# Both feed-forward products by one level of Strassen's algorithm, in two phases through device memory, on one Trainium2 core

## The chip, the core and the metric

One core of a Trainium2 chip. The metric is the device time of one execution in microseconds: the median of three runs. A separate execution was taken by the hardware profiler; its rows are what is read here. TensorE does the matmuls, VectorE and ScalarE the elementwise work and the copies out of PSUM, POOL (GpSimd) the weight sums, and SP issues nearly all transfers.

## The reference, cut to what matters

One layer of a streaming encoder: a first half (adaptive norm, input projection, pooling mixer, state-space mixer, output projection, residual), then a squared-ReLU feed-forward with its own norm and residual, then a final norm. Only the feed-forward changes:

```python
h = rms_norm(x, norm_ffn_w) * (1.0 + sc2) + sh2
f = jnp.square(jax.nn.relu(h @ w_ff1 + b_ff1)) @ w_ff2 + b_ff2
x = x + g2 * f
y = rms_norm(x, final_norm_w)
```

D_MODEL is 1024 and the feed-forward is 4096 wide. There are 2048 prompt tokens and 8 x 16 sample tokens, 2176 in all, and everything is float32.

## The kernel before, in words

**Layout and precision.** Features lie on the 128 partitions, tokens along the free dimension. Every matrix product is done in three matmuls of reduced-width operands: `mm3` (L178 to L180) multiplies the high part of the weights with the high and the low part of the data, and the low part of the weights with the high part of the data. The split of a weight tile into parts is a cast on ScalarE and a subtraction on VectorE (`wsplit`, L172 and L174; `wpair`, L952 and L954), from a raw tile that SP loads (four raw buffers, three split ones).

**Stages.** Phase A (to about 1050 us) does the first half up to the mixers. Then the output projection (`out_proj`, L827) runs over three pairs of token tiles, the last of 128-column sample tokens. In its shadow POOL computes sums and differences of the first feed-forward weights (`combine`, L853): for each of 16 units u and each half of the columns it loads four blocks (L857), does four 256-column operations (L859) and stores four results to device memory (L860), with a single buffer `pp`.

**Feed-forward.** It runs over three pairs of token tiles (364 + 364, 364 + 364, 360 + 360 columns; the last tile holds the sample tokens). A pair's two tiles are the two column halves of the Strassen scheme. `load_h` (L892) makes seven operand sets from the normed input (b11, t3, t1, t2, b21, t4, b22; four tiles each, in high and low parts). `ff1_unit` (L957) makes two feature tiles for both token tiles from seven products of 4 x 3 = 12 matmuls each, 84 in all, instead of the 96 of the plain form. Its evictions go to tiles `e` of the pool `fe`; after ReLU and square they are split again and stay in SBUF. `ff2` (L1010) is plain: for every four feature tiles it goes through eight output tiles and two token tiles with 12 matmuls each and adds the result to the residual `xs` on VectorE (L1021). The two are interleaved: two `ff1_unit`s, then one `ff2` step. After the last step come the sums of squares, `rsqrt_of` (small matmuls L237 and L260), the final scale (L1051) and the stores.

**Order.** The kernel is written in program order, with a list of small tasks (`fill`) that are dropped in between (`filler`, `drain`). A scheduler orders each engine's instructions before the run, by priority and the readiness it expects; on the chip each engine, and each DMA queue, works strictly in that order. The memory of the weight sums is given back just before the feed-forward, and the eviction tiles are placed there:

```python
    hs = load_h(SUPERS[0], rs)
    with tc.high_priority(offset=FPRIO):
        drain()
    pstack.close()
    fe = region("fe")
```

## Time and profile before

| what | value |
|---|---|
| median of three runs | 2995.47 us (2990.91 to 3008.11) |
| the profiled execution | 3008.98 us, of which the span is 3007.2 us |
| TensorE busy | 95% of the span |
| VectorE, ScalarE, POOL busy | 65%, 45%, 6% |
| mean granted TensorE clock | 0.973 |
| transfers | 433.74 MB, 144 GB/s over the span |

Busy shares are averages over stages with different limits. A busy TensorE is not one at its peak, since matmuls overlap: the distance between their starts is what one costs. A window row gives busy time and counts for one stretch; after them stand the granted clock (1.00 is the 2.4 GHz level, 0.50 the 1.2 GHz level), the mean busy share of the 16 DMA engines and GB/s.

### The profile page before, as it was taken

The numbers are of one execution on the slowest core, as the hardware profiler recorded it, in microseconds if no ns is written. First come the engines' busy times: TensorE is split into PE (matmuls) and PEld (weight loads), VectorE is DVE, ScalarE is ACT, GpSimd is POOL, SyncE is SP. The second block draws the span as 40 slices with busy tenths as digits, with TensorE's granted clock in tenths as the row PEclk, the third lists the DMA queues.
The fourth block names the chain that finished last, engine by engine and source line by source line (L and its number), as shares of the span: only waits on it lengthen the run. The fifth ranks groups of instructions, "written<-read, shape, count | busy, mean of one in ns | idle before, by whom it ended". The sixth has DMA issues, their size and how long they took to land.

```text
span 3007.2 us, 45269 instructions
## 1 busy us (share of the span) xinstructions
PE 2859.1 (95%) x17000; PEld 2742.3 (91%) x17000; DVE 1969.7 (65%) x3832; ACT 1348.3 (45%) x2518; POOL 184.2 (6%) x228
## 2 busy tenths in 40 slices
PE   7899999999999899999289999999999999999998
PEld 5799998989989799999179999999999999999997
DVE  7578796778978684643354556685555587555556
ACT  6646455544624233232253444554433465334442
POOL 0000000000000043443400000000000000000000
PEclk9999999999999999999589999999999999999999
DMA  6657443523564677876442233454323245222332
GB/s 231 184 181 220 133 126 111 147 91 119 161 163 142 159 251 247 217 241 211 147 147 91 97 109 110 125 172 134 106 95 108 93 150 171 95 92 95 112 109 76
DMA packets 293836, 433.74 MB, mean 144 GB/s; under 512 B 73008, under 2 KB 199920, under 8 KB 293616
## 3 DMA queue, kind: packets, MB, share of 16 engines
q1 hardware_dynamic: 283888, 397.28, 42.9%
q0 software_dynamic: 9728, 33.56, 3.4%
q8 instruction: 134, 2.20, 0.3%
q14 instruction: 86, 0.70, 0.1%
HBM read 364.88 MB, written 65.85 MB: 143 GB/s over the span
## 4 chain that ended last, share of the span: by engine, by line
PE 73%; DMA 9%; issue 6%; POOL 5%; DVE 4%; ACT 2%; SPq 0%; DVEq 0%; POOLq 0%; ACTq 0%
PE g L180 19%; PE g L178 19%; PE g L179 19%; DMA sD<-pp 4%; POOL pp L859 4%; PE y L180 3%; PE y L178 3%; PE y L179 3%; POOL pp L857 2%; PE y L604 1%; PE t L609 1%; PE y L602 1%; DMA sb<-h 1%; PE t L260 1%; PE t L237 1%
## 5 line engine op out<-in xcount | busy, mean ns | idle before, releaser
L178 PE MATMUL g<-h,wh 128*128 128x384 f32 (+3 forms) x2432 | 814.2, 335 | 56.0 <-ACT e L985 47.6
L179 PE MATMUL g<-h,wh 128*128 128x384 f32 (+3 forms) x2432 | 812.6, 334 | 1.8 <-DVE h L900 1.6
L180 PE MATMUL g<-h,wl 128*128 128x384 f32 (+3 forms) x2432 | 814.0, 335 | 0.0
L178 PE MATMUL g<-c,wh 128*128 128x364 f32 (+3 forms) x1792 | 592.4, 331 | 26.0 <-ACT c L899 15.9
L180 PE MATMUL g<-c,wl 128*128 128x364 f32 (+3 forms) x1792 | 593.7, 331 | 0.8 <-DVE wl L174 0.6
L179 PE MATMUL g<-c,wh 128*128 128x364 f32 (+3 forms) x1792 | 591.1, 330 | 2.3 <-DVE c L900 2.0
L178 PEld LDWEIGHTS g<-h,wh 128*128 128x128 f32 x2432 | 462.6, 190 | 69.9 <-ACT e L985 48.1
L172 ACT CAST wh<-wr 128x1024 fp32r<-128x1024 f32 x290 | 301.9, 1048 | 383.4 <-PE g L179 311.9
L179 PEld LDWEIGHTS g<-h,wh 128*128 128x128 f32 x2432 | 462.6, 190 | 12.2 <-issue 6.8
L174 DVE TENSOR_TENSOR wl<-wr,wh 128x1024 fp32r<-128x1024 f32 x290 | 355.0, 1230 | 178.8 <-ACT wh L172 169.4
L180 PEld LDWEIGHTS g<-h,wl 128*128 128x128 f32 x2432 | 462.3, 190 | 8.7 <-issue 5.9
L952 ACT CAST wh<-wr 128x1024 fp32r<-128x1024 f32 x192 | 180.9, 942 | 458.3 <-PE g L179 341.0
L178 PEld LDWEIGHTS g<-c,wh 128*128 128x128 f32 x1792 | 339.4, 189 | 30.2 <-ACT c L899 17.2
L180 PEld LDWEIGHTS g<-c,wl 128*128 128x128 f32 x1792 | 339.2, 189 | 8.8 <-DVE wl L954 4.9
L179 PEld LDWEIGHTS g<-c,wh 128*128 128x128 f32 x1792 | 339.2, 189 | 3.9 <-DVE c L900 2.9
L954 DVE TENSOR_TENSOR wl<-wr,wh 128x1024 fp32r<-128x1024 f32 x192 | 209.5, 1091 | 154.3 <-ACT wh L952 150.7
L1021 DVE SCALAR_TENSOR_TENSOR c<-g,mod,c 128x364 f32<-128x364 f32 (+2 forms) x256 | 146.0, 571 | 170.9 <-PE g L180 170.6
L178 PE MATMUL y<-c,wh 128*128 128x364 f32 (+3 forms) x608 | 200.2, 329 | 3.1 <-DVE c L1021 3.1
L180 PE MATMUL y<-c,wl 128*128 128x364 f32 (+3 forms) x608 | 200.4, 330 | 1.3 <-DVE wl L174 1.3
L179 PE MATMUL y<-c,wh 128*128 128x364 f32 (+3 forms) x608 | 199.8, 329 | 0.0
L972 ACT ACTIVATE e<-e 128x364 f32<-128x364 f32 (+1 forms) x192 | 95.1, 496 | 77.3 <-DVE e L997 72.4
L1021 DVE SCALAR_TENSOR_TENSOR c<-y,mod,c 128x364 f32<-128x364 f32 (+2 forms) x128 | 73.0, 570 | 85.8 <-PE y L180 85.5
(243 smaller groups left out, 3766.7 us busy)
## 6 DMA issues: line engine op xcount, KB each, us to landing
wr<-wf SPq DMA_DIRECT2D x108, 512.0 KB, 3.5
wr<-sD SPq DMA_DIRECT2D x192, 256.0 KB, 3.2
wr<-win SPq DMA_DIRECT2D x84, 512.0 KB, 4.0
wr<-wf SPq DMA_DIRECT2D x144, 256.0 KB, 2.9
wr<-wada SPq DMA_DIRECT2D x48, 512.0 KB, 5.1
E<-aD SPq DMA_DIRECT2D x34, 512.0 KB, 5.4
x<-xT SPq DMA_DIRECT2D x88, 192.0 KB, 3.4
pp<-wf POOLq DMA_DIRECT2D x64, 256.0 KB, 4.1
```

The source lines that it names most:

```text
L172: S.copy(wh, raw)
L174: V.tensor_tensor(wl, raw, wh.bitcast(F32), op=ALU.subtract)
L178: T_.matmul(out, lhsT=wh, rhs=ah, start=start, stop=False, skip_group_check=more)
L179: T_.matmul(out, lhsT=wh, rhs=al, start=False, stop=False, skip_group_check=more)
L180: T_.matmul(out, lhsT=wl, rhs=ah, start=False, stop=stop, skip_group_check=more)
L237: T_.matmul(pn[:, c:c + 1], lhsT=acc[:, c * P:(c + 1) * P], rhs=ones[:, 0:1], start=True, stop=True)
L857: nc.gpsimd.dma_start(w[:, 2 * i:2 * i + 2], a["wf1"][2 * u + i].rearrange("p (b x) -> p b x", b=2)[:, :, hs])
L859: nc.gpsimd.tensor_tensor(w[:, out], w[:, x], w[:, y], op=op)
L952: S.copy(wh[:, :n], raw[:, :n])
L954: V.tensor_tensor(wl[:, :n], raw[:, :n], wh[:, :n].bitcast(F32), op=ALU.subtract)
L972: S.activation(c, c, AF.Relu)
L1021: V.scalar_tensor_tensor(x1[:, :Tp], pg[:, :Tp], G[:, 0:1], x1[:, :Tp], op0=ALU.mult, op1=ALU.add)
```

## The change

The first product keeps its seven products, and the second gets the same scheme. For this the feed-forward is parted in two phases. Phase one runs all 16 units of `ff1_unit` for all three pairs. After each unit POOL forms the four differences t1 to t4 of its results, and seven tiles go to device memory (`fD`). Phase two runs, for each pair, four chunks of four units: `load_f` brings a chunk's 28 operand tiles back and splits them, and each `ff2_unit` makes seven products (84 matmuls) whose evictions are added up in SBUF over the four chunks; in the last chunk `residual` reloads x, scales and adds, and sums the squares. `final` does the last norm, its pieces mixed into the next pair's first units.

`combine` serves both weights: the second ones are summed in the first phase of pairs 0 and 1, half a unit's sums per unit. The sums' pool `pp` is a region of its own; the temporaries of the projection go to a pool `to`, whose place the eviction tiles `fe` take over. The first operand sets of pair 0 are made before the last two column tiles of the projection. In phase two POOL does the low parts of two of a unit's four weight loads. The weights are repacked on the host so that each of the four blocks of a unit is one 512-column run.

In the diff below, removed lines (the functions printed above show them) and some small helpers are left out: `hraw` loads one tile of x and norms it, `hput` splits it, `late` does both for the sets b21 and b22, `optile` and `actile` hand out tiles of three and two pools in turn.

```diff
+    def right(stack, name):
+        return stack.enter_context(tc.tile_pool(name=name, bufs=1, side="right", reuse_waits=REUSE))
+
+    cstack, ostack = ExitStack(), ExitStack()
+    cls_pool = {c: right(cstack, c) for c in ("c0", "c2")}
     tp2 = region("tpb")
+    pp = region("pp")
+    to = ostack.enter_context(tc.tile_pool(name="to", bufs=1, reuse_waits=REUSE))
...
     def tmp():
-        return tp2.tile([P, TM], F32, tag="m", name="m", bufs=3)
+        return to.tile([P, TM], F32, tag="m", name="m", bufs=3)
...
+    HOPS = ("b11", "t3", "t1", "t2", "t4", "b22", "b21")
...
+    def combine(w, u, half):
         hs = slice(256 * half, 256 * half + 256)
-        w = pool.tile([P, 4, 256], F32, tag="pp", name="pp", bufs=1)
-        for i in range(2):
-            nc.gpsimd.dma_start(w[:, 2 * i:2 * i + 2], a["wf1"][2 * u + i].rearrange("p (b x) -> p b x", b=2)[:, :, hs])
+        t = pp.tile([P, 4, 256], F32, tag="pp", name="pp", bufs=1)
+        nc.gpsimd.dma_start(t, a[w][u][:, :, hs])
         for out, x, y, op in ((3, 2, 3, ALU.add), (2, 0, 2, ALU.subtract), (0, 3, 0, ALU.subtract), (1, 1, 0, ALU.subtract)):
-            nc.gpsimd.tensor_tensor(w[:, out], w[:, x], w[:, y], op=op)
-        nc.gpsimd.dma_start(sD[u][:, :, hs], w)
+            nc.gpsimd.tensor_tensor(t[:, out], t[:, x], t[:, y], op=op)
+        nc.gpsimd.dma_start(sD[w][u][:, :, hs], t)
...
+    def wpair(pool_lo, *srcs):
...
+            eng = nc.gpsimd if pool_lo else V
+            eng.tensor_tensor(wl[:, :n], raw[:, :n], wh[:, :n].bitcast(F32), op=ALU.subtract)
...
+    def products(w, u, hs, T, after, pool_lo=()):
+        src = wset(w, u)
+        ws = {}
+        banks = {}
+        for i, n in enumerate(HOPS):
+            if i % 2 == 0:
+                names = HOPS[i:i + 2]
+                ws.update(zip(names, wpair(i // 2 in pool_lo, *(src[x] for x in names))))
+            b = {"b11": "a", "t2": "a", "t3": "c", "t4": "c", "t1": "b", "b22": "b", "b21": "d"}[n]
+            more = b in banks
+            if not more:
+                banks[b] = obank()
+            out = banks[b][:, :T]
+            wh, wl = ws[n]
+            for q in range(4):
+                sl = slice(q * P, (q + 1) * P)
+                hi, lo = hs[n][q]
+                mm3(out, wh[:, sl], wl[:, sl], hi[:, :T], lo[:, :T], q == 0 and not more, q == 3, more)
+            after(n, out)
+            filler(1)
...
+    def load_h(sup, rs, cls, temp, first):
...
+        def early(q):
+            b11, b12, b22 = hraw(sup, rs, q, 0), hraw(sup, rs, q, 1), hraw(sup, rs, q + 4, 1)
+            hput(hs, cls, "b11", q, b11, T)
+            t1 = temp()[:, :T]
+            V.tensor_tensor(t1, b12, b11, op=ALU.subtract)
...
+            if not first:
+                b21 = hraw(sup, rs, q + 4, 0)
+                V.tensor_tensor(b21, b21, t1, op=ALU.subtract)
+                hput(hs, "c1", "t4", q, b21, T)
+
+        def t4(q):
+            keep[q] = hraw(sup, rs, q + 4, 0)
+            t = temp()[:, :T]
+            hi, lo = hs["t2"][q]
+            V.tensor_tensor(t, keep[q], hi[:, :T].bitcast(F32), op=ALU.subtract)
+            V.tensor_tensor(t, t, lo[:, :T].bitcast(F32), op=ALU.subtract)
+            hput(hs, "c1", "t4", q, t, T)
...
+    def ff1_unit(n, sup, hs, u):
...
+            return fe.tile([P, TF], F32, tag="e", name="e", bufs=9)[:, :T]
...
+        def spill(name, c):
+            DQ.dma_start(fD[n][u][HOPS.index(name)], c)
...
+        def after(name, pg):
...
+            else:
+                c = e["c11"]
+                V.tensor_tensor(c, c, pg, op=ALU.add)
+                put("b11", c)
+                spill("b11", c)
+                t1, t2, t4 = (stage()[:, :T] for _ in range(3))
+                sub(t1, e["b12"], e["b11"])
+                spill("t1", t1)
+                sub(t2, e["b22"], t1)
+                spill("t2", t2)
+                sub(e["b12"], e["b22"], e["b12"])
+                spill("t3", e["b12"])
+                sub(t4, e["b21"], t2)
+                spill("t4", t4)
+
+        products("wf1", u, hs, T, after)
...
+    def load_f(n, c, T):
...
+            DQ.dma_start(raw, fD[n][4 * c + q][HOPS.index(x)])
             S.copy(hi[:, :T], raw)
             V.tensor_tensor(lo[:, :T], raw, hi[:, :T].bitcast(F32), op=ALU.subtract)
...
+    def residual(x, pgs, s, m, acc):
+        T, t0, last, Tp = fdims(s)
+        x1 = stage()
+        xcols(x1, m, t0, T)
+        G, B = MOD(5, m), g2b[:, m, :]
+        S.activation(x1[:, :Tp], x1[:, :Tp], AF.Identity, bias=B[:, 0:1])
+        V.scalar_tensor_tensor(x[:, :Tp], x[:, :Tp], G[:, 0:1], x1[:, :Tp], op0=ALU.mult, op1=ALU.add)
...
+        sq_add(tp2, acc[0], x[:, :T], T, not acc[1])
...
+    def ff2_unit(sup, hs, c, mp, A, accs):
...
+        def into(key, pg):
+            if key in A:
+                V.tensor_tensor(A[key], A[key], pg, op=ALU.add)
+            else:
+                A[key] = actile(T)
+                S.copy(A[key], pg)
...
+        def done(key, j, i):
+            if key != "c11":
+                V.tensor_tensor(A[key], A[key], A["u"], op=ALU.add)
+            residual(A[key], None, sup[j], 2 * mp + i, accs[j])
...
+        products("wf2", 4 * c + mp, hs, T, after, (1, 3))
...
-    out_proj(SUPERS[2], pin2, yin2, range(8))
+    out_proj(SUPERS[2], pin2, yin2, range(6))
     drain()
-    hs = load_h(SUPERS[0], rs)
+    hs, rest = load_h(SUPERS[0], rs, "c2", tmp, True)
+    out_proj(SUPERS[2], pin2, yin2, range(6, 8))
+    drain()
     with tc.high_priority(offset=FPRIO):
-        drain()
-    pstack.close()
+        for fn in rest:
+            fn()
+    ostack.close()
     fe = region("fe")
...
     for n, sup in enumerate(SUPERS):
         nxt = SUPERS[n + 1] if n + 1 < len(SUPERS) else []
...
+        for u in range(16):
+            if n < 2:
+                combine("wf2", 8 * n + u // 2, u % 2)
+            if u == 5 and nxt:
+                rs = load_r(nxt)
+            if u == 9:
+                drain()
+                if nxt:
+                    hn, rest = load_h(nxt, rs, "c2" if n % 2 else "c0", etmp, False)
+            ff1_unit(n, sup, hs, u)
         drain()
...
+    cstack.close()
+    opa, opb = right(ctx, "opa"), right(ctx, "opb")
+    hs, rest = load_f(0, 0, FBS[0])
+    with tc.high_priority(offset=F2PRIO):
+        for fn in rest:
+            fn()
+    for n, sup in enumerate(SUPERS):
...
+        for c in range(4):
+            nxt = (n, c + 1) if c < 3 else (n + 1, 0)
+            if nxt[0] < 3:
+                hn, rest = load_f(*nxt, FBS[SUPERS[nxt[0]][0]])
+                fill.extend(rest)
...
+            for mp in range(4):
+                ff2_unit(sup, hs, c, mp, A[mp], accs)
...
+        fin = final(sup, A, accs)
+        if n < 2:
+            drain()
+            fill[0:0] = fin
+        else:
+            for fn in fin:
+                fn()
```

## Rows read from the trace of the kernel before

**Rows 1.** The page's busy shares by engine.

```profile
PE 2859.1 (95%) x17000; PEld 2742.3 (91%) x17000; DVE 1969.7 (65%) x3832; ACT 1348.3 (45%) x2518; POOL 184.2 (6%) x228
```

**Rows 2.** Windows: busy us (x instructions) of PE, PEld, DVE, ACT, POOL; clock, DMA, GB/s.

```profile
1440.00:1470.00 30.00, 12.87 (x33) 9.21 (x33) 22.24 (x40) 13.40 (x26) 12.13 (x15) 0.50 0.56 173
1470.00:1514.00 44.00, 0.00 (x0) 0.00 (x0) 0.00 (x0) 0.22 (x1) 18.83 (x26) 0.50 0.27 93
...
1514.40:1545.00 30.60, 27.59 (x130) 25.14 (x131) 22.30 (x40) 25.99 (x55) 0.00 (x0) 0.85 0.64 186
...
1600.00:1700.00 100.00, 100.00 (x598) 99.19 (x597) 54.98 (x82) 42.63 (x76) 0.00 (x0) 1.00 0.30 98
...
1900.00:2000.00 100.00, 96.86 (x572) 95.80 (x572) 77.60 (x141) 61.67 (x115) 0.00 (x0) 0.98 0.49 149
2000.00:2100.00 100.00, 96.55 (x563) 94.56 (x561) 65.72 (x117) 50.00 (x93) 0.00 (x0) 0.98 0.49 157
...
2400.00:2500.00 100.00, 97.66 (x573) 96.28 (x573) 80.93 (x154) 62.21 (x117) 0.00 (x0) 0.98 0.45 136
2500.00:2600.00 100.00, 96.00 (x569) 94.40 (x568) 65.96 (x133) 46.89 (x87) 0.00 (x0) 0.98 0.45 145
```

**Rows 3.** Timeline of PE: start us, duration us; the feed-forward's first and last, and neighbours.

```profile
1431.46 0.33 PE L178 MATMUL g<-c,wh 128*128 128x364 f32 x1
...
1700.25 0.33 PE L178 MATMUL g<-c,wh 128*128 128x364 f32 x1
1700.41 0.33 PE L179 MATMUL g<-c,wh 128*128 128x364 f32 x1
1700.58 0.33 PE L180 MATMUL g<-c,wl 128*128 128x364 f32 x1
...
2990.59 0.33 PE L180 MATMUL y<-h,wl 128*128 128x360 f32 x1
```

**Rows 4.** Timeline of ACT around the first eviction; in brackets the idle time before it.

```profile
1513.78 0.56 ACT L985 ACTIVATE e<-g,vec 128x364 f32<-128x364 f32 x1 [48.47 <-DMA sD<-pp]
```

**Rows 5.** The tile view of `pp`: POOL's sums, and what POOL waited for.

```profile
L859 POOL TENSOR_TENSOR pp<-pp x128: 712/745/1707, 1063.9 to 1509.2; 128x256 f32<-128x256 f32 x128
...
  DMA pp<-wf: 128.6, 32
  DMA sD<-pp: 119.4, 31
```

**Rows 6.** Queues at 300:900, 1514:2000, 2000:2510, POOL's at 1050:1420: packets, MB, share.

```profile
q1 hardware_dynamic: 65995, 77.94, 44.3%
...
q1 hardware_dynamic: 35424, 56.36, 36.9%
...
q1 hardware_dynamic: 36864, 60.60, 37.5%
...
q0 software_dynamic: 7456, 25.69, 21.1%
```

**Rows 7.** Chain of waits from 1515 and at the end: start us, us, what.

```profile
1534.87 0.43 SPq L866
...
2023.50 1.14 DVE wl L954
...
2026.60 0.45 DVE acc L276
...
3000.89 3.00 DVE c L1051 x6
```

**Rows 8.** Timeline of DVE near 1450: one op beside a sum of POOL, one alone.

```profile
1446.73 1.06 DVE L294 TENSOR_TENSOR x<-x,rb 128x364 f32<-128x364 f32 x1
...
1455.96 0.53 DVE L900 TENSOR_TENSOR c<-m,c 128x364 fp32r<-128x364 f32 x1
```

**Rows 9.** Timeline of POOL: four sums beside VectorE's ops, four without.

```profile
1445.44 3.92 POOL L859 TENSOR_TENSOR pp<-pp 128x256 f32<-128x256 f32 x4 [4.95 <-DMA pp<-wf]
...
1472.20 3.12 POOL L859 TENSOR_TENSOR pp<-pp 128x256 f32<-128x256 f32 x4 [3.42 <-DMA pp<-wf]
```

More of the change, by code (lines that the diff above doesn't have):

```diff
@@ new lines, in wpair @@
+    def wpair(pool_lo, *srcs):
+        n = 512 * len(srcs)
+        with tc.high_priority(offset=WPRIO):
+            raw = wp.tile([P, 1024], F32, tag="wr", name="wr", bufs=WRB)
+            for i, src in enumerate(srcs):
+                DQ.dma_start(raw[:, 512 * i:512 * i + 512], src)
+            wh = wp.tile([P, 1024], F32R, tag="wh", name="wh")
+            S.copy(wh[:, :n], raw[:, :n])
+            wl = wp.tile([P, 1024], F32R, tag="wl", name="wl")
+            eng = nc.gpsimd if pool_lo else V
+            eng.tensor_tensor(wl[:, :n], raw[:, :n], wh[:, :n].bitcast(F32), op=ALU.subtract)
+        return [(wh[:, 512 * i:512 * i + 512], wl[:, 512 * i:512 * i + 512]) for i in range(len(srcs))]
@@ L893, in load_h, with late @@
+    def load_h(sup, rs, cls, temp, first):
         T = FBS[sup[0]]
         hs = {n: [None] * 4 for n in HOPS}
-        def put(n, q, raw):
-            cls = "c2" if n in ("b11", "t3", "t1") else "c1"
-            hi, lo = qt(cls, F32R), qt(cls, F32R)
+        keep = {}
+        def early(q):
[3 more added lines that the diff above has]
+            V.tensor_tensor(t1, b12, b11, op=ALU.subtract)
+            V.tensor_tensor(b12, b22, b12, op=ALU.subtract)
+            hput(hs, cls, "t3", q, b12, T)
+            hput(hs, cls, "t1", q, t1, T)
+            V.tensor_tensor(t1, b22, t1, op=ALU.subtract)
+            hput(hs, cls, "t2", q, t1, T)
+            if not first:
[9 more added lines that the diff above has]
+            hput(hs, "c1", "t4", q, t, T)
+        def late(n, q):
+            x = keep.pop(q, None) if n == "b21" else None
+            if x is None:
+                x = hraw(sup, rs, q + 4, 1 if n == "b22" else 0)
+            hput(hs, "c1", n, q, x, T)
+        fill.extend(lambda q=q: early(q) for q in range(4))
+        rest = []
+        if first:
+            rest += [lambda q=q: t4(q) for q in range(4)]
+        rest += [lambda n=n, q=q: late(n, q) for n in (("b21", "b22") if first else ("b22", "b21")) for q in range(4)]
+        return hs, rest
@@ new lines, in hymba_step, with optile, actile, one @@
+    nop = [0]
+    def optile():
+        i = nop[0] % 85
+        nop[0] += 1
+        if 53 <= i:
+            return htile()
+        return (opa if i < 33 else opb).tile([P, TF], F32R, tag="op", name="op", bufs=33 if i < 33 else 20)
+    nac = [0]
+    def actile(T):
+        i = nac[0] % 22
+        nac[0] += 1
+        if i < 9:
+            return fe.tile([P, TF], F32, tag="e", name="e", bufs=9)[:, :T]
+        return opb.tile([P, TF], F32, tag="ac", name="ac", bufs=13)[:, :T]
+    def load_f(n, c, T):
+        hs = {x: [None] * 4 for x in HOPS}
+        def one(x, q):
+            lo, hi = optile(), optile()
+            raw = lo[:, :T].bitcast(F32)
+            DQ.dma_start(raw, fD[n][4 * c + q][HOPS.index(x)])
@@ new lines, in one @@
+            hs[x][q] = (hi, lo)
+        return hs, [lambda x=x, q=q: one(x, q) for x in HOPS for q in range(4)]
+    def residual(x, pgs, s, m, acc):
[5 more added lines that the diff above has]
+        V.scalar_tensor_tensor(x[:, :Tp], x[:, :Tp], G[:, 0:1], x1[:, :Tp], op0=ALU.mult, op1=ALU.add)
+        if last:
+            V.tensor_tensor(s3(x[:, Tp:T]), s3(x[:, Tp:T]), strm(G), op=ALU.mult)
+            V.tensor_tensor(s3(x1[:, Tp:T]), s3(x1[:, Tp:T]), strm(B), op=ALU.add)
+            V.tensor_tensor(x[:, Tp:T], x[:, Tp:T], x1[:, Tp:T], op=ALU.add)
+        sq_add(tp2, acc[0], x[:, :T], T, not acc[1])
+        acc[1] = True
@@ new lines, in final, with diag, rows, out @@
+    def final(sup, xs, accs):
+        rs = [None] * len(sup)
+        def diag(j):
+            rs[j] = rsqrt_diag(tp2, accs[j][0], FBS[sup[j]], 1.0 / D, EPS)
+        def rows(j):
+            rs[j] = rsqrt_rows(tp2, rs[j], FBS[sup[j]], direct=sup[j] == FLAST)
+        def out(j, k):
+            T, t0, last, Tp = fdims(sup[j])
+            x = xs[k // 2][f"c{k % 2 + 1}{j + 1}"]
+            V.scalar_tensor_tensor(x, x, VC("fnw", k), rs[j][:, :T], op0=ALU.mult, op1=ALU.mult)
+            DQ.dma_start(o["yT"][:, k, t0:t0 + T], x)
+        js = range(len(sup))
+        return [lambda j=j: diag(j) for j in js] + [lambda j=j: rows(j) for j in js] + \
+               [lambda j=j, k=k: out(j, k) for k in range(KT) for j in js]
@@ L1058, in hymba_step @@
     drain()
-    pstack = ExitStack()
-    pp = pstack.enter_context(tc.tile_pool(name="pp", bufs=1))
     for u in range(16):
         for half in range(2):
-            combine(pp, u, half)
+            combine("wf1", u, half)
     pin1 = in_pool(SUPERS[1], "c2")
```

237 lines of the change are left out of this document (77 added, 160 removed).

## Prediction

> **What bounds the kernel now.** First the busy shares of the page: TensorE has matmuls in flight for 95% of the span [rows 1], so time comes off by fewer matmuls or by closing the few holes, and not by lighter work elsewhere. Then the windows, to find the holes [rows 2]. The reader is to see three kinds of stretch. In a steady one (1600 to 1700) TensorE starts 598 matmuls in 100 us at full clock, VectorE is busy 55 us of it and the DMA engines 0.30. In the hole at the start of the feed-forward (1440 to 1545) there are 33, 0 and 130 matmuls in 30, 44 and 30.6 us, at clock 0.50, 0.50 and 0.85 (0.50 is the 1.2 GHz level). At the two seams between token pairs the counts are 572, 563, 573 and 569. Third the timeline of TensorE, for the price of a matmul [rows 3]: 364-column ones start 0.1667 us apart, so 360-column ones are put at 0.165 by their width.
>
> The feed-forward's matmuls are 3 x 16 x 84 = 4032 in the first product and 3 x 128 x 12 = 4608 in the second; a third of each is 360 wide. That is 5760 x 0.1667 + 2880 x 0.165 = 1435 us. The stretch runs from 1431.5 to 2990.9 [rows 3], 1559 us, so 124 us are lost: 86 at the start (166 matmuls, 27.7 us of work, in the 113.5 us up to 1545), 19 at the two seams (115 matmuls fewer than four times 598), and 19 elsewhere, mostly the norms' own small matmuls.
>
> The start is explained by one wait. ScalarE's first eviction stands 48.5 us until the weight sums' store has landed [rows 4]: its tile `e` lies in the memory that the sums' pool gave back, and the sums run on POOL till 1509, one half-sum per 14.3 us, half of it waits for its own load (128.6 us over 32) and store (119.4 over 31), since there is one buffer [rows 5].
>
> **The change, part by part.** The sum goes against the profiled execution's 3009.0 us (span 3007.2); the median of the runs is 2995.5, 0.9955 of it.
>
> *Fewer matmuls.* The second product gets seven in place of eight: 16 x 84 per pair, 4032 instead of 4608. 8064 matmuls take 5376 x 0.1667 + 2688 x 0.165 = 1340 us: **-96 us**, all on the path.
>
> *The start.* The sums' pool stands by itself now, so no eviction waits for it; the sums themselves run as late as before, but unit u needs only its own, done by about 1064 + 28.6 x (u + 1), and starts at 1431 + 14 x u or later. The first four operand sets are made during the last two column tiles of the output projection (28 us of matmuls); only t4, b21 and b22 come during the first unit. What is late next is that chain: four tiles through a load, two passes on each of two engines. I take 20 us lost (bounds 5 and 35) for 86: **-66**.
>
> *First product, DMA.* A unit lasts 84 x 0.1667 = 14.0 us. From the windows' queue rows [rows 6] a packet costs the engines 64.4 ns at a mean of 1181 bytes and 81.0 at 1591 (4253 and 2869 engine-us), so 16.6 ns + 0.0405 ns per byte; the third window (83.0 at 1644) agrees within 0.3. A unit then needs: seven weight loads of 128 rows of 2048 bytes, 89 engine-us; the new spills, seven of 128 rows of 1456 bytes, 68; in pairs 0 and 1 half a sum of the second weights, 0.52 MB in and 0.52 out at POOL's rate (1249 engine-us for 25.69 MB), 51; and from unit 5 on the next pair's x, 40 tiles in two pieces each over 11 units, 43. Together 208, or 13.0 us on 16 engines, in the first five units, and 251, or **15.7 us**, in the other eleven: more than the 14.0 of TensorE. That is 1.7 x 11 x 2 = 38 us, if no other traffic could wait.
>
> *First product, VectorE and POOL.* Starts of VectorE's ops are 0.45 apart for 364 columns, 0.50 with a scalar operand and 1.14 for a 1024-wide weight split [rows 7]. A unit has five of the short ones (2.4 us), three and a half splits (4.0) and, in the eleven units, 3.8 us of the next pair's operands: 10.2 us. POOL adds four sums and four differences, 4 x 0.745 [rows 5] and, by width, 4 x 1.06 us. Beside POOL's ops a VectorE op of 0.53 us lasts 1.06, and POOL's four last 3.92 instead of 3.12 [rows 8, 9]. If every POOL op lengthens one op so, VectorE loses 4 x 0.53 + 4 x 0.75 = 5.1 us, if six in ten, 3.1: 13.3 to 15.3 us of 14.0. ScalarE, with 11 passes of at most 0.56 [rows 4], casts no dearer than the splits and 2.4 us of operands, stays near 12.6. SP issues 14 transfers and 7 pieces at 0.43 [rows 7], 9 us; the spills stand in its queue ahead of weight loads and wait for POOL's differences, and what covers that are the four raw and three split weight buffers, two products (4 us) each. DMA and VectorE both come to about 15.5, at the same units, so I take the DMA's 38 and a third more for its not being full all the time: **+50** (0 if the sums and x loads spread into idle time; 110 if these units take 18 and the others 15).
>
> The Trainium skill speaks against this use of POOL. In "SBUF — State Buffer", section "Who interferes with whom", a VectorE instruction with two SBUF inputs and a GpSimd one that reads SBUF exclude each other for the whole instruction. The rows show one op of each started every 0.98 us (3.92 / 4) where one after the other would be 0.45 + 0.80, so I stay with the rows; the rule taken whole is a rival below.
>
> *Second product.* DMA is 89 + 68 per unit, 9.8 us: covered. VectorE has seven evictions, seven operand splits and two weight splits, 8.6 us, and 0 to 3.2 for POOL's split of the others (2.98 and 1.49 us by width from 0.745): covered by 14.0 in three of four chunks. In the last chunk the residual, its squares and three sums add 5.2: 13.8 to 17.0, and nothing covers it. Eight units (pair 2 has no next operands) x 1.6 on the mean, and slack of two banks: **+15** (0 to 40).
>
> *Seams.* Five now (two between pairs in each half, one between the halves) for two at 9.6 each; the accumulators of the next pair wait for output stores, but TensorE runs on for a unit's two spare banks. I put 5 each, 25 for 19: **+6** (-19 to +31). *Tail:* both tiles of the pair now finish together, so eight more output ops of 0.50 follow the last matmul: **+4** (0 to 10). Repacking weights on the host costs nothing here.
>
> Sum: -96 - 66 + 50 + 15 + 6 + 4 = -87, so 2922 profiled, and x 0.9955 = **2909 us**. With all lower bounds 2800, with all upper ones 3039.
>
> **The rivals.**
> 1. *All keeps up.* Sums, spills and residuals lie in idle time and both terms of stretched units are nothing: 2909 - 65 = 2844. For it: before, at a DMA share of up to 0.49 and VectorE at 81, a seam loses only 5%. Against: 15.7 us of DMA in 14.0.
> 2. *Whole lock.* VectorE and POOL exclude each other for each whole op: 10.2 or 6.4 own plus 7.2 of POOL, 16.2 on the mean in 32 units (+70), 18.3 in eight and 15.1 in four last-chunk units (+39). 109 for 65: 2953. For it: both engines' ops lengthen; against: the 0.98.
> 3. *POOL is the bound; slower.* In the order written, a half-sum and four differences take POOL 0.7 + 4.0 + 3.1 + 0.8 + 4.2 to 5.6, just a unit, if the differences run while the store lands. If loaded DMA queues keep both waits uncovered, a unit of pairs 0 and 1 lasts the old 14.3 plus 5.1 = 19.4 us, the tiles `e` come free late and evictions stand: 5.4 x 32 = 173 for 50, 3032. It decides from about 18 us a unit on.
> 4. *The start does not get better.* The tiles `e` now lie over the temporaries of the projection, and the t4 chain uses those; if the first eviction waits for all of it and for POOL's slow loads, the 66 are not won: 2975.
>
> **How the numbers follow.** Chances: forecast 0.46 (own range 2865 to 2955), rivals 0.20, 0.15, 0.10, 0.09. A measurement of this kernel tells about 0.5% (15 us) from no change. Slower is rival 3, 0.10; within 0.5% falls what is left at the upper edges of the forecast, 2 and 4, 0.06; faster 0.84. The range goes from below rival 1 to above 2 and 4, **2835 to 3000**; rival 3 and the lowest bounds are left out.
>
> **What would show it.** Right: 576 fewer matmuls; no wait of the first eviction on the sums' store; DMA share over 0.9 in pairs 0 and 1 of the first product, and over 14.0 us per unit there against 14.0 in pair 2; VectorE nearly full in the last chunks. Wrong: units of 14.0 us everywhere (rival 1); TensorE waiting for evictions that wait for POOL's differences (rival 3); VectorE without idle time at a DMA share below 0.8 (rival 2); a hole of over 40 us near 1430 (rival 4).

## The result and the profile after

The changed kernel takes 3338.1 us (median of 4 runs, 3324.5 to 3346.1) against 2997.0 before on the same chip: ratio 1.113, 95% interval 1.108 to 1.118. It is slower by 11%. The forecast was 2909, and the measured time lies far outside its range.

The page after, the lines that answer to [rows 1], and its queue:

```profile
span 3344.0 us, 47389 instructions
...
PE 2883.3 (86%) x16424; PEld 2719.4 (81%) x16424; DVE 2119.2 (63%) x3860; ACT 1539.9 (46%) x2874; POOL 723.5 (22%) x676
...
POOL 0000000000023333344455232233321211212221
PEclk9999999999999999985678899899998988979988
...
q1 hardware_dynamic: 419248, 557.28, 54.6%
```

There are 576 matmuls fewer, as meant, but TensorE is busy for 86% of the span in place of 95%, and no other engine or queue comes near its full share. The time went into waits, then. Windows after, with the columns of [rows 2]:

```profile
1500.00:1550.00 50.00, 8.99 (x54) 8.69 (x53) 3.59 (x4) 4.83 (x9) 18.39 (x25) 0.62 0.30 101
1550.00:1600.00 50.00, 0.00 (x0) 0.00 (x0) 0.00 (x0) 0.00 (x0) 20.99 (x29) 0.50 0.25 87
...
1700.00:1800.00 100.00, 57.17 (x274) 53.84 (x272) 35.25 (x53) 31.88 (x63) 51.12 (x57) 0.75 0.66 209
...
2300.00:2400.00 100.00, 98.24 (x597) 97.34 (x596) 53.97 (x67) 60.23 (x108) 35.25 (x31) 1.00 0.75 239
...
2700.00:2800.00 100.00, 79.51 (x363) 70.36 (x362) 71.52 (x135) 48.39 (x93) 16.53 (x9) 0.80 0.64 197
```

The reader is to see two troubles. From about 1509 to 1640 TensorE stands while POOL alone works; from there to 1850 it has about half its matmuls. At the end of the first product (2300 to 2400) it starts 597 in 100 us, as many as a steady stretch before had. In the second product it has stretches such as 2700 to 2800 with 363. To measure both, these rows give the first eviction of the first product (L1015), the last unit's first difference (L1010) and the second product's last matmul into the PSUM tile `g` (L182; the very last, into `y`, starts 2 us later, at 3320.5); behind the count stand least, median and greatest ns, then the first and last start in us:

```profile
L1015 ACT ACTIVATE e<-g,vec x32: 537/546/567, 1471.7 to 2421.2; 128x364 f32<-128x364 f32 x22, 128x360 f32<-128x360 f32 x10
...
L1010 POOL TENSOR_TENSOR x<-e x48: 949/1055/1430, 1637.5 to 2450.9; 128x364 f32<-128x364 f32 x32, 128x360 f32<-128x360 f32 x16
...
L182 PE MATMUL g<-h,wl x2317: 277/334/745, 50.9 to 3318.6; 128*128 128x384 f32 x112, 128*128 128x364 f32 x39, 128*128 128x256 f32 x22, 128*128 128x360 f32 x21
```

So the first product lasts 2450.9 - 1471.7 = 979 us and the second 868, for 4032 matmuls each, which take 670 us at full clock: 309 and 198 us are lost. The first eviction starts at 1471.7 instead of 1513.8 [rows 4], and after the start of the very last matmul come 24 us instead of 17. The differences between the two executions add up: -42 at the start, +7 at the end, and 1849 us from first eviction to last matmul instead of 1477, together 337 us, as the spans say.

**Where TensorE stands in the first product.** First the waits of TensorE from 1465 to 2450 (total us, times, longest), then ScalarE's timeline, then POOL's:

```profile
PE g L180 <- ACT e L1018: 153.0, 3, 132.1
```

```profile
1503.73 0.55 ACT L1015 ACTIVATE e<-y,vec 128x364 f32<-128x364 f32 x1
...
1640.45 0.56 ACT L1018 ACTIVATE e<-g,vec 128x364 f32<-128x364 f32 x1 [134.97 <-POOL e L1010]
```

```profile
1629.47 3.12 POOL L868 TENSOR_TENSOR pp<-pp 128x256 f32<-128x256 f32 x4 [3.24 <-DMA pp<-wf]
1633.00 0.74 POOL L869 DMA_DIRECT2D sDwf<-pp  x1 [0.40 <-POOL pp L868]
1636.74 0.77 POOL L866 DMA_DIRECT2D pp<-wf  x1 [3.00 <-DMA sDwf<-pp]
1637.52 0.97 POOL L1010 TENSOR_TENSOR x<-e 128x364 f32<-128x364 f32 x1
...
1896.53 1.07 POOL L1010 TENSOR_TENSOR x<-e 128x364 f32<-128x364 f32 x1 [8.16 <-ACT e L1003]
...
1910.54 1.08 POOL L1010 TENSOR_TENSOR x<-e 128x364 f32<-128x364 f32 x1 [9.58 <-ACT e L1003]
```

A matmul waits 132 us for an eviction (L1018), the eviction 135 us for a tile `e`, and the tile for the first unit's differences on POOL. The unit's last square (L1003) had ended at 1491.9; POOL had 50 half-sums in its order ahead of the difference of 1637.5, the 32 of the first weights and 18 of the second ones, one every 11.1 us where nothing else runs. The program writes one half-sum of the second weights ahead of each unit; on the engine the scheduler had put 18 there, since their tile and their data were free and the differences' were not. Up to 1842 the other 14 lie between the differences, and the differences come 20 to 32 us apart. Then the sums are done and the differences come 14.0 us apart (1896.53, 1910.54): TensorE is the bound again, at a DMA share of 0.75.

**In the second product** no wait of TensorE is longer than 3.4 us. The windows of a chunk's seam, and two neighbouring matmuls in it:

```profile
2500.00:2510.00 10.00, 10.00 (x62) 9.99 (x60) 4.19 (x5) 4.74 (x9) 2.41 (x1) 1.00 0.54 166
2510.00:2520.00 10.00, 8.41 (x51) 8.13 (x50) 4.89 (x8) 6.14 (x12) 1.46 (x2) 1.00 0.68 226
2520.00:2530.00 10.00, 5.99 (x31) 4.73 (x29) 6.20 (x8) 3.26 (x7) 3.51 (x2) 0.95 0.57 181
2530.00:2540.00 10.00, 6.82 (x17) 4.85 (x18) 6.14 (x12) 5.08 (x10) 0.00 (x0) 0.50 0.69 216
2540.00:2550.00 10.00, 8.15 (x27) 6.27 (x25) 5.59 (x12) 4.82 (x10) 0.00 (x0) 0.70 0.64 220
2550.00:2560.00 10.00, 7.83 (x28) 7.43 (x29) 5.26 (x6) 3.24 (x6) 2.37 (x1) 0.66 0.29 90
```

```profile
2531.30 0.67 PE L180 MATMUL g<-op,wh 128*128 128x364 f32 x1 [2.68 <-ACT op L1079]
...
2538.61 0.51 PE L181 MATMUL y<-op,wh 128*128 128x364 f32 x1
2538.91 0.50 PE L182 MATMUL y<-op,wl 128*128 128x364 f32 x1
```

Of 62 matmuls in 10 us first 51 and 31 and then some 17 to 28 are left: operands come late, TensorE makes short stops, and the granted clock falls to 0.50, where starts are 0.30 us apart instead of 0.1667 [rows 3]. What the reads stand behind is seen in SP's timeline and in its waits from 2445 to 3325:

```profile
2516.45 0.38 SPq L1078 DMA_DIRECT2D op<-fD  x1
2522.26 0.80 SPq L881 DMA_DIRECT2D wr<-sDwf  x2
```

```profile
SPq L881 <- POOL wl L886: 297.4, 89, 9.6
SPq L881 <- DVE wl L886: 144.2, 66, 5.9
```

The reads of the operands (L1078) stand in SP's order behind weight loads (L881) that wait till POOL has made a low part (L886); ahead of the load at 2522.26 SP stood 5.4 us for one. Such waits alone do not show a loss: in e7_opmajor below SP waits 268 us for VectorE's low parts in the same place, and the phase is 156 us shorter.

### The profile page after: what moved, and what is told of

Read it like the earlier page. It is cut to its first block, busy times and chain, and to the rows that moved or that the text cites. A ratio compares the mean times of both kernels' runs of the same rounds, so it can differ in the third digit from the quotient of the medians.

```text
span 3344.0 us, 47389 instructions
## 1 busy us (share of the span) xinstructions
PE 2883.3 (86%) x16424; PEld 2719.4 (81%) x16424; DVE 2119.2 (63%) x3860; ACT 1539.9 (46%) x2874; POOL 723.5 (22%) x676
## 5 line engine op out<-in xcount | busy, mean ns | idle before, releaser
L182 PE MATMUL g<-h,wl 128*128 128x384 f32 (+3 forms) x2317 | 783.8, 339 | 1.2 <-POOL wl L886 1.2
L886 DVE TENSOR_TENSOR wl<-wr,wh 128x1024 fp32r<-128x1024 f32 (+1 forms) x288 | 374.2, 1300 | 265.7 <-ACT wh L883 244.3
L883 ACT CAST wh<-wr 128x1024 fp32r<-128x1024 f32 (+1 forms) x384 | 358.8, 938 | 342.0 <-PE g L181 189.5
L182 PEld LDWEIGHTS g<-h,wl 128*128 128x128 f32 x2317 | 446.9, 193 | 10.8 <-issue 5.9
L886 POOL TENSOR_TENSOR wl<-wr,wh 128x1024 fp32r<-128x1024 f32 x96 | 184.7, 1924 | 683.7 <-ACT wh L883 573.9
L866 POOL DMA_DIRECT2D pp<-wf x64 | 49.4, 771 | 1185.2 <-PE t L589 947.3
L180 PE MATMUL g<-c,wh 128*128 128x364 f32 (+3 forms) x768 | 263.1, 343 | 39.2 <-ACT e L1015 13.5
L176 DVE TENSOR_TENSOR wl<-wr,wh 128x1024 fp32r<-128x1024 f32 x182 | 225.8, 1250 | 110.4 <-ACT wh L174 99.9
L174 ACT CAST wh<-wr 128x1024 fp32r<-128x1024 f32 x182 | 188.5, 1047 | 223.1 <-PE g L181 186.2
L868 POOL TENSOR_TENSOR pp<-pp 128x256 f32<-128x256 f32 x256 | 230.4, 900 | 266.5 <-DMA pp<-wf 251.5
L182 PE MATMUL g<-c,wl 128*128 128x364 f32 (+3 forms) x768 | 261.9, 341 | 16.2 <-DVE wl L886 12.1
L181 PE MATMUL g<-c,wh 128*128 128x364 f32 (+3 forms) x768 | 261.9, 341 | 2.3 <-DVE c L949 1.6
L180 PE MATMUL g<-op,wh 128*128 128x364 f32 (+1 forms) x563 | 194.9, 348 | 25.5 <-ACT op L1079 16.2
L181 PE MATMUL g<-op,wh 128*128 128x364 f32 (+1 forms) x565 | 196.1, 349 | 13.9 <-DVE op L1080 13.8
L182 PE MATMUL g<-op,wl 128*128 128x364 f32 (+1 forms) x563 | 191.8, 343 | 0.8 <-POOL wl L886 0.8
L180 PEld LDWEIGHTS g<-c,wh 128*128 128x128 f32 x768 | 150.9, 197 | 44.9 <-ACT e L1015 15.5
```

The costliest lines, as they stand in the source:

```text
L174: S.copy(wh, raw)
L176: V.tensor_tensor(wl, raw, wh.bitcast(F32), op=ALU.subtract)
L180: T_.matmul(out, lhsT=wh, rhs=ah, start=start, stop=False, skip_group_check=more)
L181: T_.matmul(out, lhsT=wh, rhs=al, start=False, stop=False, skip_group_check=more)
L182: T_.matmul(out, lhsT=wl, rhs=ah, start=False, stop=stop, skip_group_check=more)
L866: nc.gpsimd.dma_start(t, a[w][u][:, :, hs])
```

## The experiments

Two theories were put first: POOL's order in the first product, and late operands at the seams of the second. The phases are read from the same rows as above; e2, e3, e11 and e12 are single runs, the others medians; the phases are those of one execution each. Runs that leave a phase as it was give 961 to 982 us for the first product and 854 to 875 for the second, so differences of some 20 us between two phases are not read. Where an expectation names L857 to L861 for a half-sum, these are the lines of the kernel before; in the changed one they are L866 to L869.

| kernel | us | first eviction at | first product | second product |
|---|---|---|---|---|
| changed | 3338.1 | 1471.7 | 979 | 868 |
| e1_pin | 3187.8 | 1460.5 | 847 | 854 |
| e2_nosum2 | 3100.9 | 1449.4 | 755 | 869 |
| e3_noreload | 3188.0 | 1468.3 | 974 | 720 |
| e4_dvelow | 3252.0 | 1460.8 | 977 | 789 |
| e6_early | 3166.0 | 1512.0 | 751 | 875 |
| e7_opmajor | 3175.3 | 1470.1 | 982 | 712 |
| e9_defer | 3181.4 | 1461.8 | 825 | 869 |
| e10_all | 2992.1 | 1511.7 | 748 | 715 |
| e11_noarith | 3137.0 | 1456.7 | 788 | 865 |
| e12_nodma | 3108.9 | 1457.5 | 762 | 862 |
| e13_best | 2968.6 | 1494.2 | 737 | 709 |
| e14_oppool | 3246.1 | 1473.5 | 961 | 792 |

**POOL's order (e1_pin).**

```diff
-            if n < 2:
-                combine("wf2", 8 * n + u // 2, u % 2)
-            ff1_unit(n, sup, hs, u)
+            last = ff1_unit(n, sup, hs, u)
+            if n < 2:
+                with tc.issue_after(last):
+                    combine("wf2", 8 * n + u // 2, u % 2)
```

> Edit: the half-sum of the second weights (L857 to L861) is handed to POOL only after the last difference (L1010) of the unit ahead of it; nothing else changes, no work is left out. Theory P (POOL's order): in the changed kernel POOL did 14 half-sums of the second weights, 11.1 us each, between 1464 and 1637 us, ahead of the first unit's differences, and the evictions' nine tiles waited for those. With the order turned round no POOL instruction of a unit stands behind more than one half-sum: the first-product phase falls from 985 us to 700 to 750, the time from 3338 to about 3080 (3050 to 3110), and the first L1010 runs before 1500 us instead of at 1637.5. Rival C (contention: VectorE and POOL hold each other up, or the DMA queue is full, whatever the order): the same instructions run beside the same others, so the gain is under 60 us (3280 or more).

3187.8 us, 1.063 of before (1.060 to 1.067). The wait of 132 us is gone, the first difference runs at 1476, and 132 us come off the first product. The order was the largest single cause in the first product, but half of the expected gain did not come: the phase is 847 us, not 700 to 750.

**No second sums (e2_nosum2).** In `wset` the first weights' sums are read for both products, and the call of `combine("wf2", ...)` is gone.

> Edit: the 32 half-sums of the second weights are left out altogether, with their loads and stores; the second product takes the first weights' stored sums in their place, so the same bytes are read back and the output is not the reference's. Theory P: nearly what the reordering alone gives, since the sums themselves fit beside 14 us units: about 3050 us (3020 to 3090), at most 40 us below the reordered kernel. Rival C (the sums' traffic and POOL's use of the memory cost the time, not their place in the order): over 100 us faster than the reordered kernel.

3100.9 us, 87 less than e1_pin. Between the two bounds set: even in good order the sums cost some 90 us of the first product. What remains without them, 755 for 670, no run took apart, but this run's trace shows where it lies. Counted by 84 matmuls a unit, TensorE takes 14.0 us for 19 of the 32 units of pairs 0 and 1. The seventh to eleventh unit of these two pairs take 14 to 34 us, 66 over, and the first two units of all three pairs together 25 over. In the long ones the next pair's x is read and its operands are made, which the program starts at the sixth and the tenth unit. In pair 0's eleventh, 31 us long, VectorE is busy 29.11 of 30 us, and 82 of some 180 matmuls start:

```profile
1600.00:1630.00 30.00, 17.85 (x82) 16.41 (x81) 29.11 (x55) 24.39 (x48) 4.48 (x4) 0.83 0.59 179
```

**Operands kept (e3_noreload) and no low parts on POOL (e4_dvelow).**

```diff
-            if nxt[0] < 3:
+            if c == 3 and nxt[0] < 3:
...
-            hs = hn
+            if c == 3:
+                hs = hn
```

> Edit: in the second product the operands are loaded and split only for chunk 0 of each pair and used again for chunks 1 to 3, so 12 of 16 operand sets (28 loads, 28 copies, 28 subtractions each) are left out and the output is not the reference's; matmuls, weights and evictions stay. Theory L (operands late at the seams, and the half clock after each): the second-product phase falls from 874 us to 690 to 740, the time from 3338 to about 3180 (3150 to 3210). Rival V (VectorE and POOL full in the last chunk, where no operand load is the reason): the phase keeps at least 820, the time 3285 or more.

```diff
-        products("wf2", 4 * c + mp, hs, T, after, (1, 3))
+        products("wf2", 4 * c + mp, hs, T, after)
```

> Edit: all low parts of the second product's weights (L886) go to VectorE; POOL makes none of them. Rival S (POOL's low parts, 1.9 us each beside VectorE's 2.2 us, hold up VectorE and the weight loads, and through SP's order the operand loads queued behind those): over 60 us faster, 3278 or less. Theory L: what is late is the operands' tiles, which come free only in a chunk's last unit; the time stays within 30 us of 3338.

3188.0 and 3252.0 us (the latter 1.084 of before, 1.080 to 1.088). The operands' reads and splits, which e3_noreload both leaves out, cost 148 of the 198 us lost, as theory L has it. But the second run refutes theory L's claim on POOL: 79 us of the phase go with its low parts, inside what rival S asked for. The two overlap, since together they are more than 198. A stretch without reads, in e3_noreload, beside the same one of the changed kernel:

```profile
2510.00:2610.00 100.00, 100.00 (x603) 100.00 (x602) 45.53 (x68) 27.71 (x31) 27.10 (x15) 1.00 0.43 141
```

```profile
2510.00:2610.00 100.00, 86.14 (x440) 79.45 (x438) 58.52 (x89) 41.36 (x73) 20.72 (x11) 0.88 0.59 187
```

With 15 low parts on POOL and no operand to split, TensorE starts 603 matmuls: here the low parts by themselves cost nothing, and what they cost elsewhere they cost together with the reads and splits.

**The sums at the program's start (e6_early).** `pp` is opened ahead of all phases, `EB = 4` becomes 3, and all 64 calls of `combine` stand ahead of the first phase.

> Edit: all 64 half-sums are handed to POOL at the program's start, where it has nothing else to do, so that none is left when the first product begins; their tile gets a place of its own through the whole program, for which the tile class E of the state-space part goes from four buffers to three. Nothing is left out. Theory P with its remainder R (each half-sum ahead of a unit's differences also makes SP's stores, and the weight loads queued behind them, late): as without the second weights' sums, 3100 us, first-product phase about 750 us. Rival A (the part ahead of 1050 us pays for it, by DMA share or by VectorE and POOL side by side): the first product starts more than 40 us later than at 1465 us and the time is 3140 or more.

3166.0 us (1.055, 1.052 to 1.058): the first product lasts 751 us, as without sums, but begins at 1512. Rival A is right too: the early part is 40 us longer. Whether their traffic or the fourth tile `E` does it, this run does not tell.

**The second product turned (e7_opmajor).** The loops in outline (the run takes the same order from a list):

```diff
-        for c in range(4):
-            for mp in range(4):
-                ff2_unit(sup, hs, c, mp, A[mp], accs)
+        for name in ("b11", "t2", "t3", "t4", "t1", "b22", "b21"):
+            for c in range(4):
+                ff2_group(sup, ready[g], name, c, A, banks, accs)
```

In `ff2_group` four banks stay open over the four chunks, so that each is evicted once a pair instead of once a chunk; the reads of the operands run eight groups ahead, and VectorE makes all low parts.

> Edit: the second product's loops are turned: for each of the seven operands all four chunks and all four output pairs, accumulated in four PSUM banks over the whole inner length, so that an operand tile is used for 8 us and freed, the reads spread evenly instead of coming in bursts at chunk seams, and each bank is evicted once a pair instead of once a chunk; low parts on VectorE alone. Same matmuls, same reads. The first product is as in the changed kernel. Theory L+S (operands late at seams, POOL's low parts beside VectorE's): the second-product phase falls from 874 us to 680 to 710, the time from 3338 to 3160 (3140 to 3180). Rival (the phase is held by the sum of its traffic and its splits, wherever they lie): the phase stays above 780 us, the time above 3240.

3175.3 us (1.057, 1.055 to 1.059): 163 us less, the phase is 712 us with the same reads, so neither the traffic's sum nor the number of splits held it, but their bunching, and POOL's low parts. The run also makes fewer evictions; no run parts that from the spreading, but in e3_noreload TensorE is full with the evictions of every chunk. Here the seam's windows are gone; at 2700 to 2800, against 363 matmuls and clock 0.80 above:

```profile
2700.00:2800.00 100.00, 100.00 (x591) 99.68 (x591) 63.28 (x104) 53.13 (x90) 0.00 (x0) 0.98 0.78 242
```

**Stores one unit later (e9_defer).** On e1_pin, to explain its other 90 us: `spill` of the four differences is put off and called in the next unit at t3.

> Edit: the reordered kernel (second weights' half-sums behind each unit's differences) with one thing more: the four stores of a unit's differences are issued in the next unit, after its first operand's product, instead of at once. Theory R (SP issues in order, and its stores wait up to 6.3 us for differences that stand behind a half-sum, with the next weights' loads behind them): the first product loses 40 to 85 us less, 3188 becomes 3105 to 3150. Rival E (what is late is the eviction tiles, which the differences free, so moving the stores changes nothing or holds one tile longer): 3170 or more.

3181.4 us (1.058, 1.057 to 1.060). Theory R falls: 6 us of 87. In the phases 22 us come off the first product and 15 are added to the second, which the edit does not touch; both are about what unchanged phases differ by. SP's order is not what the sums cost.

**All repairs (e10_all).** e6_early, e9_defer's stores and e7_opmajor in one.

> Edit: all repairs together: the half-sums at the program's start, the differences' stores one unit later, the second product operand by operand with low parts on VectorE. Nothing is left out. If the losses found are all there are, the first product takes 720 to 755 us from 1465 us, the second 680 to 710, and the end 15 to 20: 2925 us (2890 to 2960), under the kernel before the change. If a loss comes back elsewhere (the early part, or the DMA queue with all reads evenly spread), 2980 or more.

2992.1 us (0.996, 0.994 to 0.997), level with the kernel before: a miss by 67 us, of which the late start makes 47 (1511.7 for 1465), as e6_early had shown it. The products are at the upper end of what was expected, or just above it (748 of 720 to 755, 715 of 680 to 710).

**What in a half-sum costs (e11_noarith, e12_nodma).** Both on e1_pin:

```diff
-            nc.gpsimd.tensor_tensor(t[:, out], t[:, x], t[:, y], op=op)
+            if w == "wf1":
+                nc.gpsimd.tensor_tensor(t[:, out], t[:, x], t[:, y], op=op)
```

> Edit: the reordered kernel without the arithmetic of the second weights' half-sums: each still loads its 512 KB and stores them, but the four POOL additions (L859) are left out, so the output is not the reference's. Of the 87 us that the second weights' sums still cost in the reordered kernel (3188 against 3101 without them), theory D (the DMA queue: 0.75 of it for a 14 us unit is 10.5 us, a half-sum's 1 MB some 3.7 us more, together 14.2, which is over the unit) expects nearly all to stay: 3165 to 3190. Theory A (POOL's arithmetic, and VectorE beside it) expects most to go: 3125 or less.

```diff
-        nc.gpsimd.dma_start(sD[w][u][:, :, hs], t)
+        if w == "wf1":
+            nc.gpsimd.dma_start(sD[w][u][:, :, hs], t)
```

(and the load only once)

> Edit: the counterpart: the reordered kernel with the second weights' four additions a half-sum kept on POOL, behind each unit's differences, but without their loads and stores (one tile is used again; the second product reads the first weights' stored sums, so the output is not the reference's). Theory D: nearly all of the 87 us go, 3100 to 3125. Theory A: most stay, 3160 or more.

3137.0 and 3108.9 us: of the 87 us, 51 go without the arithmetic and 79 without the transfers. Neither theory holds, since neither part is the bound: the chain of both is. POOL's timeline in e1_pin, one unit:

```profile
1479.89 0.79 POOL L866 DMA_DIRECT2D pp<-wf  x1
1487.34 3.63 POOL L868 TENSOR_TENSOR pp<-pp 128x256 f32<-128x256 f32 x4 [6.65 <-DMA pp<-wf]
1491.37 0.75 POOL L869 DMA_DIRECT2D sDwf<-pp  x1 [0.40 <-DMA wr<-sDwf]
1492.09 1.04 POOL L1010 TENSOR_TENSOR x<-e 128x364 f32<-128x364 f32 x1
1493.21 0.98 POOL L1010 TENSOR_TENSOR x<-e,x 128x364 f32<-128x364 f32 x1
1494.14 1.96 POOL L1010 TENSOR_TENSOR e<-e 128x364 f32<-128x364 f32 x1
1496.06 1.27 POOL L1010 TENSOR_TENSOR x<-e,x 128x364 f32<-128x364 f32 x1
1497.28 0.78 POOL L866 DMA_DIRECT2D pp<-wf  x1
```

Load, wait, four sums, store, four differences: 17.4 us in this unit, 15.8 on the mean of the four between the differences of 1476.00 and 1539.17, with nothing in POOL's queue to fill its wait for the load. Against 14.0 that is 1.8 x 32 = 58 us, and by 59 the first product gets shorter in e11_noarith, where the chain is 3.6 us shorter and so under the unit. This is an estimate: it takes four units for all 32, of which some ten are held up without any sums too (e2_nosum2), so that it meets the 59 so closely is partly luck. The other 33 of 92 us are left for the transfers, which is argued and not shown; the DMA share is 0.90 in e11_noarith at 1500 to 1550 and 0.77 in e12_nodma.

**The best of it (e13_best).** e10_all with the first weights' sums back where the change had them, and the second weights' 32 begun once the first of the three passes of the early part is through.

```diff
             h = super_a(sup, h, SUPERS[i + 1] if i + 1 < len(SUPERS) else [], mg)
+            if i == 0:
+                for u in range(32):
+                    combine("wf2", u // 2, u % 2, None if u else h[0][0][0][:, 0:1].bitcast(F32))
```

> Edit: the kernel with all repairs, but the first weights' half-sums are back where the change had them (from about 1050 us, ahead of the first product) and the second weights' 32 come once the first of the three passes of the part ahead is through, so that they lie over the stretch in which the DMA queue is least used, away from the first 200 us. Nothing is left out. Theory A2 (half-sums cost the early part time mainly by their reads in the first 200 us and by DMA share near 0.8 later): the first product starts by 1480 us instead of 1505, the time falls from 2992 to 2965 (2950 to 2980). Rival (the fourth tile of class E is what the early part misses, or any half-sum there costs the same): 2985 or more.

2968.6 us, 0.990 of before (0.989 to 0.992): faster than both kernels, by 1.0% and 11%. The time is within what theory A2 gave, but its reason is shown in half at most: the first eviction comes at 1494, not by 1480, which is 17 us earlier than in e10_all and not 25. The profiled executions differ by 33 us, and the other 16 lie in the two products, of which the theory said nothing. Against 1471.7 some 22 us of the early part are still lost, and whether to the half-sums or to the fourth tile `E` stays open.

**POOL's low parts without seams (e14_oppool).**

```diff
-            ws = wpair(False, *(wset("wf2", 4 * c + mp)[name] for mp in (2 * h, 2 * h + 1)))
+            ws = wpair(h == 1 and name != "b21", *(wset("wf2", 4 * c + mp)[name] for mp in (2 * h, 2 * h + 1)))
```

> Edit: the kernel with the second product's loops turned, with one thing put back: three sevenths of its weights' low parts are made by POOL again (the second of two weight pairs, but for the last operand), as many as the change put there. Nothing is left out. Making all low parts on VectorE took 86 us off the changed kernel, letting operands stay took 150, both with the turned loops 163, so the two overlap. Theory O (POOL's low parts cost only because VectorE and SP were already late at the chunk seams): without seams they cost under 20 us, 3165 to 3195. Theory K (they cost in themselves, since VectorE and POOL lengthen each other's instructions everywhere): 50 us or more, 3225 and up.

3246.1 us (1.084, 1.081 to 1.087), 71 more than e7_opmajor; the second product takes 792 us for 712. The time is theory K's. By form, 2500 to 3100, first VectorE's operand splits in e7_opmajor, then the same and POOL's low parts in e14_oppool (busy us, mean ns, idle time ahead):

```profile
L1082 DVE TENSOR_TENSOR op<-op 128x364 fp32r<-128x364 f32 x113 | 60.2, 536 | 62.1 <-ACT op L1081 61.7
```

```profile
L1082 DVE TENSOR_TENSOR op<-op 128x364 fp32r<-128x364 f32 x111 | 95.1, 864 | 95.7 <-ACT op L1081 95.5
...
L886 POOL TENSOR_TENSOR wl<-wr,wh 128x1024 fp32r<-128x1024 f32 x54 | 129.9, 2406 | 470.8 <-ACT wh L883 298.8 <-DVE ac L1130 45.1 <-DMA wr<-sDwf 30.4
```

A low part that VectorE makes in 1.22 us takes POOL 2.41, and the mean split lasts 0.86 us instead of 0.54. The mean hides two kinds. Of the 181 splits of 364 columns in this stretch 145 ran beside no low part and last 0.53 us on the mean; the other 36 last 2.16, and 35 of these end 0.39 to 0.40 us after the low part beside them. One such pair, POOL's timeline and VectorE's:

```profile
2503.01 2.36 POOL L886 TENSOR_TENSOR wl<-wr,wh 128x1024 fp32r<-128x1024 f32 x1 [7.50 <-ACT wh L883]
```

```profile
2503.36 2.40 DVE L1082 TENSOR_TENSOR h<-h 128x364 fp32r<-128x364 f32 x1 [0.81 <-ACT h L1081]
```

The split starts 0.35 us behind the low part, stands until that has ended at 2505.37, and ends at 2505.76: VectorE is shut out for all the rest of POOL's instruction. So theory K names the right engines, but they do not lengthen each other everywhere: a low part that meets no VectorE instruction takes 2.40 us as well, and a split is longer only where it meets one. Nor do the low parts cost the time in themselves, as e3_noreload showed: with them and without the reads the phase is 720 us, with the reads and without them 712, with both 792. How much of the 80 us is this lock stays open. The waits that the trace lists for TensorE are 39 us for POOL's low parts (L182 on L886, 24.8 and 13.8) and 3 us for a split.

## Why the prediction was wrong

*Fewer matmuls, -96:* right, 576 fewer, and where nothing holds it TensorE starts 597 in 100 us.

*The start, -66:* right in kind. No eviction waits for the sums' store; the first comes 42 us earlier in the changed kernel and 64 us earlier in e2_nosum2. Rival 4 did not come.

*First product, +50 (0 to 110):* this is the step that failed; it measures +309. The prediction costed each engine's work per unit, a half-sum and four differences on POOL "in the order written". It never asked in what order POOL would have them. The half-sums of the second weights depend on nothing in the unit, so a scheduler that fills an idle engine took 18 of them ahead of the first differences, and the engine cannot overtake. e1_pin shows the cost of that order alone: 132 us. Of the rest, 92 go with the sums (e2_nosum2), and 85 remain without the sums; no run took these apart, and by e2_nosum2's trace most of them lie where the next pair's operands are made. The sum put that work at 3.8 us of VectorE a unit, spread over eleven units; on the chip it came bunched in a few, with VectorE full.

*Rival 3* (POOL is the bound, tiles `e` come free late, 3032) named the right place and the right tiles, at 0.10. Its price was too low for the same reason: it put 19.4 us into every unit, where POOL held back the first unit for 135 us and then took 20 to 32 us for each. In good order its lower figure was nearer: 15.8 us, as "just a unit" of 14 plus the load's wait, 6.65 in the unit shown instead of 4.0 [rows 5]. That the DMA sum gave 15.7 too is chance: it held for units with the next pair's x, and the row is from units without.

*Second product, +15, and the seams in it:* they measure +198 together, the second step that failed. "DMA is 9.8 us a unit: covered" is a mean over a chunk. A chunk holds 56 of 85 operand tiles, so about half of the next chunk's can be read ahead; the others come free only in the chunk's last unit, and reads and splits come together (23 reads in the 33 us of the second chunk's first unit, 0 to 9 in each of the three behind it); e7_opmajor has the same reads spread out and takes 712 us. POOL's low parts were put at 0 to 3.2 us of VectorE per unit and taken as covered; e4_dvelow and e14_oppool show 79 and 80 us of phase. VectorE was not full in the last chunks (0.79 of 2660 to 2736, the first pair's), and the DMA share stayed at 0.76 or less in every 100 us of the first product: two of the four signs for the forecast did not appear, and one of those against it did, evictions that wait for POOL's differences.

*Rival 2* (VectorE and POOL exclude each other) was weighed by short operations, 0.98 us for one of each. The Trainium skill, "SBUF — State Buffer", section "Who interferes with whom", has such a pair block each other for a whole instruction. The trace agrees: a split that meets one of POOL's 2.41 us operations ends 0.39 us after it. Already the forecast's own rows say so, and it read them wrongly. POOL's additions before and after VectorE's 1.06 us at 1446.73 [rows 8]:

```profile
1446.49 0.91 POOL L859 TENSOR_TENSOR pp<-pp 128x256 f32<-128x256 f32 x1
...
1447.48 0.90 POOL L859 TENSOR_TENSOR pp<-pp 128x256 f32<-128x256 f32 x1
```

VectorE's instruction ends at 1447.79, 0.39 us after the first addition, and the second addition ends 0.59 us after that. One behind the other is 0.39 + 0.59 = 0.98, the very number that the forecast took for side by side; the 0.45 and 0.80 that it added up are the distances at which either engine starts its own instructions, and are longer than what one holds up the other. Rival 2 had the mechanism right, then. Its price, 109 us, went to units of the first product, where units beside the differences alone run in 14.0 us (e2_nosum2), and to the last chunks; the other chunks, which it took as covered, lost time too.

*Tail, +4:* +7.

## What to carry to other kernels

Work that is handed to an idle in-order engine has a place in its queue, and that place is set by when its inputs are ready, not by where it is written: look at what it can overtake, and tie it behind what others wait for. Cost a phase by when its buffers come free, not by its mean: the second product took 868 us with its reads in bursts and, with the same reads spread out and the low parts off POOL, 712. A saving of 96 us in matmuls was worth 1% once these waits were out of the way.

## What was not expected of the hardware

VectorE and POOL shut each other out: a split of VectorE takes 0.53 us alone and 2.16 on the mean where it meets one of POOL's 2.41 us instructions, since it ends 0.39 us after that one, however early it started. A mean over all splits (0.86) hides this, and so does a row in which both engines' instructions are short.

Short stops cost more than their length. In the second product TensorE's waits sum to 106 us, none longer than 3.4, and 198 us are lost: behind the stops of a seam the granted clock went from 1.00 to 0.50 within 30 us, and matmuls started 0.30 us apart. Neighbours that start 0.22 to 0.36 us apart (358, counted in the trace) make up 45 us of the difference; the rest was not taken apart.

A half-sum came every 11.1 us from POOL where the other engines stood, and every 11.5 to 20.7 us beside them; its four additions took 3.12 us there, and up to 6.47 (at 1463, with VectorE at work). Its length in quiet is no measure of what a unit has to cover.
